# A decoder layer on one core: the merge of the attention heads as four pairs of seven block products, with the weights' sums and the split w_out made ahead

## The chip, the cores and the metric

The kernel runs on one core of one Trainium2 chip. The metric is device time in microseconds (us): the median of the runs of the whole program, all stages in one launch. Five engines work side by side on that core, each through its own queue of instructions in order: TensorE (PE, matrix products; PEld is its loading of stationary blocks), VectorE (DVE), ScalarE (ACT), GpSimd (POOL) and SyncE (SP, which here only issues DMAs). Matrix products accumulate in PSUM banks of 128 x 512 floats; everything else lives in SBUF, 128 partitions wide, and in device memory (the tiles whose names end in `_d`).

## The reference

One layer, 1024 tokens, width 1024, float32 throughout. What matters here is the middle of it:

```python
proj = h @ w_in                                  # q, k, v, pooled branch, memory query, gate logits
a = diff_attention(q_d, k_d, v_d, lam)           # 8 heads of 128 channels
a = rms_norm(a, subln_g) * (1.0 - lam_init)      # per head
y_attn = a.reshape(B, S, 1024) @ w_attn_branch   # "the merge of the heads"
...
gates = sigmoid(gate_logits).reshape(B, S, 3, D)
mix = gates[:, :, 0] * y_attn + gates[:, :, 1] * y_pool + gates[:, :, 2] * y_mem
x = x + rms_norm(mix @ w_out, norm_mix_post)
h2 = rms_norm(x, norm_ffn_pre)                   # then w_up, a causal conv, gelu, w_down
```

## The kernel before

Products are made in float32 precision out of three passes: each operand is split into a high part (`F32R`, the rounded value) and a low part (the rest), and `mm3` (L102) issues high x high, high x low, low x high. `split` (L85) is one ACT copy and one DVE subtraction. Activations are held transposed: channels on the 128 partitions, tokens along the row, in two halves of H = 512 tokens.

Several large products already use a scheme of seven block products in place of eight: a product of a 2 x 2 block matrix of weights by a 2 x 2 block matrix of activations (two halves of the contracted channels, two halves of the tokens) is made of seven products of sums of blocks. `seven` (L198) does so for a pair of 128-channel output tiles: `weight_sums` (L184) makes four sums of weight blocks on DVE, `product` (L175) splits one 128 x 512 block of weights into a page (tags `wh` and `wl`, two of each, so four pages) and runs 4 x 3 matmuls with one of the operands B11, T1, T2, B22, T3, B21, T4; results are combined as the banks `pa`, `pb`, `pc` are emptied.

The order of the work is not that of the source alone. A planner goes through all instructions with a cost model before the program is built; on each engine it takes, among those that it believes ready, the one written earliest. `tc.issue_after(ins)` puts what follows behind `ins` on its engine. Tiles rotate in pools by tag, so an instruction also waits until the tile whose place it takes has been read for the last time. Once the order is fixed, each engine keeps it on the chip: an instruction that waits holds up all behind it on that engine. The same holds for the DMA issues on SP.

The stages that the change touches, in order:

- **The mix gates' stage** (L860 to L881). For four pairs of output tiles and two branches, `seven` makes gate logits from the stream's operands; the sigmoid is multiplied with `y`, a branch's output that was loaded from memory, and the sum goes to `mixp_d`. Tag `y` has two places of 8 KB a partition. The weights come as two raw tiles an iteration (L868).
- **The attention** (L1156 and on), heads in turn. `weigh_values` sends each head's output to `ao_d`, `head_norm` its sum of squares to `ss_d`; `turn_sums` (L1243) sends the softmax sums to `sum_d`. For heads 4 to 7 `load_norms(1)` (L1251) reads both back, `head_norms(1)` (L1258) makes the norm factors on DVE in small steps and writes `r_d`. Meanwhile PE makes the last three tiles of attention gate logits (`gate`, L1112, dt 5 to 7).
- **The merge.** For each head the loop at L1373 loads its output `a` and its norm factors `rb`, spread over all partitions, multiplies them (L1384) and splits the result into `ath`, `atl`. `merge_heads` (L1356) makes an output tile of 128 channels: 8 heads x 3 matmuls for each half of the tokens; the first two tiles take heads 0 to 3 while heads 4 to 7 still come in. `merge` (L1403) multiplies with the gate, adds `mixp_d` and splits the result into `mixh`, `mixl`. `load_wo` (L1396) loads and splits w_out's eight row blocks.
- **The w_out stage** (L1482). For eight tiles of 128 tokens, 8 x 2 x 3 matmuls, then both norms, then the rows are turned and, for the second half of the tokens, the feed-forward operands B21 and B11 are split (`early_operands`, L1453).
- **The feed-forward's first products** (`early_products`, L1533), which need only B21; the other operands are made meanwhile (`late_operands`, L1466).

## Time and profile before

| | |
|---|---|
| median of three runs | 1726.82 us (1725.88 to 1727.25) |
| span of the profiled execution (its only time) | 1727.6 us |
| PE busy | 1712.8 us, 99% |
| DVE, ACT, POOL busy | 1241.3, 886.6, 45.0 us |
| mean TensorE clock granted | 0.999 |
| matmuls of the merge (tile pya) | first at 910.8 us, last at 997.6 us |
| w_out's matmuls (tile pout) | first at 997.9 us, last at 1090.1 us |
| DMA moved | 294.41 MB, mean 170 GB/s |

In the profile, L12 is line 12 of the kernel before, `out<-in` names tiles by the program's names, and times of places are counted from the start of the span. A group's row gives durations of one instruction (min/median/max in ns) and the first and the last start. Matmuls are pipelined: one takes longer from start to end than the step from one to the next. What stands in square brackets on a row of the timeline is how long the engine sat idle before it and what released it. "DMA to landing" is the time from the issue to the last byte.

### The profile page before, as it was taken

What the parts mean: (1) busy time and instruction counts of PE and PEld (TensorE: products, weight loads), DVE (VectorE), ACT (ScalarE), POOL (GpSimd) and SP (SyncE); (2) the same over time, 40 slices, a digit from 0 to 9 for tenths busy, and PEclk for the clock granted to TensorE, in tenths of its full rate; (3) what the DMA queues carried; (4) which work ended last, traced back from release to release, by engine and by line L of the source; (5) the groups of instructions that cost most, each with busy time, mean ns of one, the idle gap of its engine ahead of it and who ended that gap; (6) DMA issues with size and microseconds to landing.
All of it is one profiled execution on the core that took longest, in us unless ns stands there. A gap on an engine that the chain in (4) does not pass through costs nothing.

```text
span 1727.6 us, 22400 instructions
## 1 busy us (share of the span) xinstructions
PE 1712.8 (99%) x8106; PEld 1421.4 (82%) x8106; DVE 1241.3 (72%) x2047; ACT 886.6 (51%) x1577; POOL 45.0 (3%) x103
## 2 busy tenths in 40 slices
...
PEclk9999999999999999999999999999999999999999
...
GB/s 273 317 281 114 163 150 133 166 147 143 266 237 159 201 231 170 176 182 152 145 187 239 176 230 50 171 225 92 124 112 107 122 85 98 190 299 106 107 149 142
DMA packets 232803, 294.41 MB, mean 170 GB/s; under 512 B 15865, under 2 KB 161526, under 8 KB 230006
## 3 DMA queue, kind: packets, MB, share of 16 engines
...
q8 instruction: 64, 1.05, 0.3%
q14 instruction: 45, 0.37, 0.1%
q10 hardware_dynamic: 16, 0.00, 0.0%
...
## 4 chain that ended last, share of the span: by engine, by line
PE 91%; DVE 5%; DMA 2%; ACT 1%; issue 1%; SPq 0%; DVEq 0%; ACTq 0%
PE pa L103 8%; PE pa L104 8%; PE pa L105 8%; PE pb L103 5%; PE pb L104 5%; PE pb L105 5%; PE pss L1161 3%; PE poa L1217 2%; PE pd L103 2%; PE pd L105 2%; PE pd L104 2%; PE pe L105 2%; PE pe L104 2%; PE pe L103 2%; PE pout L103 2%; PE pout L105 2%
## 5 line engine op out<-in xcount | busy, mean ns | idle before, releaser
L89 ACT ACTIVATE wpage<-s 128x512 fp32r<-128x512 f32 x136 | 85.3, 627 | 108.2 <-DVE s L188 35.3
L90 DVE TENSOR_TENSOR wpage<-s,wpage 128x512 fp32r<-128x512 f32 x136 | 92.8, 688 | 43.2 <-ACT wpage L89 43.2
L1565 DVE SCALAR_TENSOR_TENSOR cvt<-gv,cols,cvt 128x1023 f32<-128x1023 f32 x88 | 112.5, 1278 | 15.6 <-ACT cvt L1561 14.9
L1165 DVE CUSTOM_DVE_ANT_0 z<-pss,hbias 128x256 f32<-128x256 f32 (+7 forms) x128 | 94.5, 752 | 26.0 <-PE pss L1161 24.8
L1170 ACT ACTIVATE z<-z,mx 128x256 f32<-128x256 f32 (+7 forms) x128 | 98.8, 773 | 20.8 <-DVE mx L1165 20.7
L103 PE MATMUL pa<-T,wpage 128*128 128x512 f32 x264 | 102.8, 389 | 0.0
L105 PE MATMUL pa<-T,wpage 128*128 128x512 f32 x264 | 102.7, 389 | 0.0
L104 PE MATMUL pa<-T,wpage 128*128 128x512 f32 x264 | 102.7, 389 | 0.0
L1161 PE MATMUL pss<-ks,q 128*128 128x512 f32 (+5 forms) x384 | 86.6, 349 | 1.4 <-DVE mx L1165 1.4
L89 ACT ACTIVATE page<-blk 128x1024 fp32r<-128x1024 f32 (+1 forms) x42 | 41.4, 989 | 85.7 <-PE pe L104 50.6
L90 DVE TENSOR_TENSOR page<-blk,page 128x1024 fp32r<-128x1024 f32 (+1 forms) x42 | 47.5, 1130 | 38.1 <-ACT page L89 38.1
L1161 PEld LDWEIGHTS pss<-ks,q 128*128 128x128 f32 x384 | 62.9, 189 | 11.1 <-DVE mx L1165 6.2
L103 PE MATMUL pd<-page 128*128 128x512 f32 x176 | 68.7, 390 | 0.0
L104 PE MATMUL pd<-page 128*128 128x512 f32 x176 | 68.5, 389 | 0.0
L105 PE MATMUL pd<-page 128*128 128x512 f32 x176 | 68.3, 389 | 0.0
L103 PE MATMUL pa<-hT,wpage 128*128 128x512 f32 x168 | 65.5, 390 | 0.1
L105 PE MATMUL pa<-hT,wpage 128*128 128x512 f32 x168 | 65.4, 389 | 0.0
L104 PE MATMUL pa<-hT,wpage 128*128 128x512 f32 x168 | 65.4, 389 | 0.0
L1217 PEld LDWEIGHTS poa<-aT,v 128*128 128x128 f32 x480 | 60.7, 190 | 3.0 <-ACT srow L1237 1.4
L1217 PE MATMUL poa<-aT,v 128*128 128x256 f32 (+1 forms) x480 | 62.5, 280 | 0.0
L103 PEld LDWEIGHTS pa<-T,wpage 128*128 128x128 f32 x264 | 49.6, 188 | 10.7 <-DVE gv L250 0.3
L104 PEld LDWEIGHTS pa<-T,wpage 128*128 128x128 f32 x264 | 49.6, 188 | 10.2
...
## 6 DMA issues: line engine op xcount, KB each, us to landing
...
wd<-in_w_down_dram SPq DMA_DIRECT2D x22, 512.0 KB, 5.0
tw_d<-wd SPq DMA_DIRECT2D x11, 1024.0 KB
rawv<-in_w_up_dram SPq DMA_DIRECT2D x22, 512.0 KB, 5.8
rawu<-in_w_up_dram SPq DMA_DIRECT2D x22, 512.0 KB, 4.1
ff_d<-cvt SPq DMA_DIRECT2D x22, 512.0 KB, 5.4
blk<-ff_d SPq DMA_DIRECT2D x20, 512.0 KB, 7.9
br<-tw_d SPq DMA_DIRECT2D x20, 512.0 KB, 5.0
```

Source lines behind the costliest of these rows:

```text
L89: copy = nc.scalar.activation(out=hi, in_=src, func=AF.Copy)
L90: nc.vector.tensor_tensor(out=lo, in0=src, in1=hi.bitcast(F32), op=ALU.subtract)
L103: nc.tensor.matmul(o, ah, bh, start=first, stop=False, skip_group_check=onto)
L104: nc.tensor.matmul(o, ah, bl, start=False, stop=False, skip_group_check=onto)
L105: return nc.tensor.matmul(o, al, bh, start=False, stop=last, skip_group_check=onto)
L1161: last["scores"] = nc.tensor.matmul(pss[:, i * H:i * H + m], q[:, j, c, ts], keys, start=(j == 0), stop=(j == 1))
L1165: nc.vector.tensor_tensor_reduce(out=halves(z[:, 0:n]), in0=pss.rearrange("p (a m) -> p a m", a=2)[:, 0:parts, 0:m], in1=halves(biases[h][ ...
L1170: nc.scalar.activation(out=z[:, 0:n], in_=z[:, 0:n], func=AF.Exp, scale=-1.0, bias=mx[:, c:c + 1], accum_out=sm if c else sums[:, h, t:t + 1])
L1217: nc.tensor.matmul(po[:, qs], (vh, vl)[i][:, k, :], w[j][:, ws], start=(n == 0), stop=(n == len(terms) - 1))
L1565: nc.vector.scalar_tensor_tensor(out=cv[:, sh:], in0=u[:, 0:S - sh], scalar=w, in1=cv[:, sh:], op0=ALU.mult, op1=ALU.add)
```

## The change

The merge becomes, for each of four pairs of output tiles, seven block products over heads 0 to 3 and 4 to 7 and over the two halves of the tokens: B11 and T1 (of heads 0 to 3 alone), T2, B22, T3, B21, T4. `merge_begin` runs the first two products of a pair, `merge_rest` the other five. Three pairs begin before anything of heads 4 to 7 is used. The operands are made head by head from the normed outputs: 28 splits of 128 x 512 where there were 16 halves, and sixteen subtractions, eight on DVE and eight on POOL. The loads of `a` and `rb` for heads 0 to 3 now stand ahead of `load_norms(1)`; for heads 4 to 7 `rb` has one place, and `a` shares six places with heads 0 to 3.

The four sums of blocks of w_attn_branch that a pair needs (`merge_sums`), and w_out's split parts (`split_wo`), are made in the gates' stage and written through POOL's DMA queue to `mw_d` and `wo_d`; both take places of tag `y`. The merge reads its sums, and the w_out stage its split parts, back from there. `mix` is kept as f32 and split tile by tile in the w_out stage. There, B11's split moves from `early_operands` to `late_operands`. The `sum_d` write moves from SP to ACT.

```diff
@@ -318,6 +318,8 @@
     wk_d = dram.tile([NH, P, 2, KT, P], F32, name="wk_d")
     v_d = dram.tile([NH, P, 2, KT, P], F32, name="v_d")
     tw_d = dram.tile([CH, P, 2, 2, H], F32, name="tw_d")
+    mw_d = dram.tile([H4, P, 4, H4, P], F32, name="mw_d")
+    wo_d = dram.tile([KT, P, 2, D], F32, name="wo_d")
     ss_d = dram.tile([NH, S], F32, name="ss_d")
...
@@ -859,6 +861,28 @@
     bstack.close()
     with tc.tile_pool(name="gp", reuse_waits="tile", bufs=2, side="right") as gp_:
+        def split_wo(k):
+            w = gp_.tile([P, 2, D], F32R, tag="y", name="wo")
+            raw = w[:, 1].bitcast(F32)
+            nc.sync.dma_start(out=raw, in_=w_out[k * P:(k + 1) * P, :])
+            split(w[:, 0], w[:, 1], raw)
+            nc.gpsimd.dma_start(out=wo_d[k], in_=w.bitcast(F32))
+        def merge_sums(p):
+            m = gp_.tile([P, 4, H4, P], F32, tag="y", name="ms")
+            for e in range(2):
+                nc.sync.dma_start(out=m[:, 2 * e:2 * e + 2].rearrange("p a k c -> p (a k) c"),
+                                  in_=chunk(w_attn_branch, (2 * p + e) * P))
+            a11, a12, a21, a22 = [m[:, j] for j in range(4)]
+            for o, x0, x1, op in ((a22, a21, a22, ALU.add), (a21, a11, a21, ALU.subtract),
+                                  (a11, a22, a11, ALU.subtract), (a12, a12, a11, ALU.subtract)):
+                nc.vector.tensor_tensor(out=o, in0=x0, in1=x1, op=op)
+            nc.gpsimd.dma_start(out=mw_d[p], in_=m)
+        ahead_of_merge = {0: (0, "0"), 1: (1, 2), 2: (3, "1"), 3: (4, "2"), 4: (5, 6), 5: (7, "3")}
         for dt in range(0, KT, 2):
             mix = None
             for b in (1, 0):
@@ -874,6 +898,8 @@
                 seven(raws, (s12[:, 0], s12[:, 1], s43[:, 0], s43[:, 1]), hop, g)
                 sigmoid = nc.scalar.activation(out=g, in_=g, func=AF.Sigmoid)
                 nc.vector.tensor_tensor(out=g, in0=g, in1=y, op=ALU.mult)
+                for what in ahead_of_merge.get(dt + 1 - b, ()):
+                    merge_sums(int(what)) if isinstance(what, str) else split_wo(what)
                 if b == 1:
                     mix = g
                 else:
@@ -1246,13 +1272,14 @@
...
-        nc.sync.dma_start(out=sum_d[g * HG:(g + 1) * HG].rearrange("h (t p) -> (h t) p", p=P), in_=row)
+        nc.scalar.dma_start(out=sum_d[g * HG:(g + 1) * HG].rearrange("h (t p) -> (h t) p", p=P), in_=row)
     def load_norms(g):
         st = small.tile([P, 4, HG, 8], F32, tag="hn", name="hn", bufs=1)
         for src, r in ((ss_d, 0), (sum_d, 3)):
-            nc.sync.dma_start(out=st[:, r], in_=src[g * HG:(g + 1) * HG].rearrange("h (p f) -> p h f", f=8))
+            with tc.issue_after(marks["head"].ins) if g else nullcontext():
+                nc.sync.dma_start(out=st[:, r], in_=src[g * HG:(g + 1) * HG].rearrange("h (p f) -> p h f", f=8))
         hns[g] = st
     def head_norms(g):
@@ -1342,84 +1369,202 @@
...
+    cstack.close()
+    dstack = ExitStack()
+    sub = dstack.enter_context(tc.tile_pool(name="sub", reuse_waits="tile", bufs=6, side="right"))
+    opr = dstack.enter_context(tc.tile_pool(name="opr", reuse_waits="tile", bufs=1, side="right"))
+    estack = ExitStack()
+    ope = estack.enter_context(tc.tile_pool(name="ope", reuse_waits="tile", bufs=1, side="right"))
+    mops = {}
+    def operands(pool, names, tag=None):
+        for n in names:
+            mops[n] = pool.tile([P, 2, H4, H], F32R, tag=tag or n, name="m" + n)
+    def mop(n, k):
+        return mops[n][:, 0, k, :], mops[n][:, 1, k, :]
+    def split_mop(n, k, src):
+        split(*mop(n, k), src)
+    operands(ope, ("B11", "T1"))
+    operands(opr, ("B22", "T2"))
+    rstack = ExitStack()
+    rbp = rstack.enter_context(tc.tile_pool(name="rbp", reuse_waits="tile", bufs=4, side="left"))
+    gs = sub.tile([P, 1], F32, name="gs", bufs=1)
+    nc.vector.tensor_scalar(out=gs, in0=cols[:, 1, 44:45], scalar1=1.0 - LAM_INIT, scalar2=None, op0=ALU.mult)
+    heads = {}
+    def load_head(h):
+        a = sub.tile([P, S], F32, tag="a", name="a")
+        nc.sync.dma_start(out=a, in_=ao_d[h])
+        rb = (rbp if h < H4 else sub).tile([P, S], F32, tag="rb", name="rb", bufs=4 if h < H4 else 1)
+        marks["head"] = nc.sync.dma_start(out=rb, in_=r_d[h:h + 1, :].partition_broadcast(P))
+        heads[h] = a, rb
+    def normed_head(h):
+        if h not in heads:
+            load_head(h)
+        a, rb = heads[h]
+        with tc.issue_after(ends["square"].ins):
+            nc.vector.scalar_tensor_tensor(out=a, in0=a, scalar=gs, in1=rb, op0=ALU.mult, op1=ALU.mult)
+        heads[h] = a[:, 0:H], a[:, H:S]
+    def upper_operands(k):
+        b11, b12 = heads[k]
+        split_mop("B11", k, b11)
+        nc.vector.tensor_tensor(out=b12, in0=b12, in1=b11, op=ALU.subtract)
+        split_mop("T1", k, b12)
+    def lower_operands(k):
+        (b11, t1), (_, b22) = heads[k], heads[H4 + k]
+        split_mop("B22", k, b22)
+        nc.vector.tensor_tensor(out=b22, in0=b22, in1=t1, op=ALU.subtract)
+        split_mop("T2", k, b22)
+    def third_operand(k):
+        (b11, _), (_, t2) = heads.pop(k), heads[H4 + k]
+        nc.gpsimd.tensor_tensor(out=b11, in0=t2, in1=b11, op=ALU.subtract)
+        split_mop("T3", k, b11)
+    def last_operands(k):
+        b21, t2 = heads.pop(H4 + k)
+        split_mop("B21", k, b21)
+        nc.gpsimd.tensor_tensor(out=b21, in0=b21, in1=t2, op=ALU.subtract)
+        split_mop("T4", k, b21)
+    for k in range(H4):
+        load_head(k)
     load_norms(1)
-    cstack.close()
...
-            split(ath[h], atl[h], a)
+    for dt in range(5, KT):
+        for step in steps(gate(dt), 8):
+            step()
+    for k in range(H4):
+        normed_head(k)
+        upper_operands(k)
+    with tc.issue_after(ends["square"].ins):
+        head_norms(1)
+    for k in range(2):
+        normed_head(H4 + k)
+        lower_operands(k)
+    rstack.close()
     hstack.close()
     mstack = ExitStack()
     mpool = mstack.enter_context(tc.tile_pool(name="mh", reuse_waits="tile", bufs=4, side="left"))
-    mixh = [mpool.tile([P, KT, H], F32R, tag="big", name="mixh%d" % i) for i in range(2)]
-    mixl = [mpool.tile([P, KT, H], F32R, tag="big", name="mixl%d" % i) for i in range(2)]
+    mix = [mpool.tile([P, KT, H], F32, tag="big", name="mix%d" % i) for i in range(2)]
+    operands(mpool, ("B21", "T4"), "big")
     wostack = ExitStack()
+    operands(wostack.enter_context(tc.tile_pool(name="opt", reuse_waits="tile", bufs=1, side="left")), ("T3",))
+    HALVES = {"B11": 0, "B21": 1, "T4": 3}
+    SUMS = {"T2": 0, "B22": 1, "T3": 2, "T1": 3}
+    def merge_weights(p, names):
+        w = wst.tile([P, 2, H4, P], F32, tag="raw", name="rawm", bufs=2)
+        for j, n in enumerate(names):
+            if n in SUMS:
+                src = mw_d[p, :, SUMS[n]]
+            else:
+                e, part = divmod(HALVES[n], 2)
+                src = w_attn_branch[part * H:part * H + H, (2 * p + e) * P:(2 * p + e + 1) * P].rearrange(
+                    "(k p) c -> p k c", p=P)
+            nc.sync.dma_start(out=w[:, j], in_=src)
+        return {n: w[:, j] for j, n in enumerate(names)}
+    def corners(p):
+        return [mix[i][:, 2 * p + e, :] for e in range(2) for i in range(2)]
+    pas = {}
+    def merge_begin(p):
+        if p == 2:
+            both = bank2(name="pm")
+            pa, pb = both[:, 0:H], both[:, H:2 * H]
+        else:
+            pa, pb = pbank(name="pm"), bank(name="pm")
+        pas[p] = pa, pb
+        c11, _, c21, _ = corners(p)
+        ws = merge_weights(p, ("B11", "T1"))
+        product(ws["B11"], mop, "B11", pa)
+        nc.scalar.activation(out=c11, in_=pa, func=AF.Copy)
+        product(ws["T1"], mop, "T1", pb)
+        nc.scalar.activation(out=c21, in_=pb, func=AF.Copy)
+    def gated(p, e, i, c, src=None):
+        hs = slice(i * H, (i + 1) * H)
+        gm = sub.tile([P, 2, H], F32, tag="a", name="gm")
+        nc.sync.dma_start(out=gm[:, 0], in_=gate_d[2 * p + e][:, hs])
+        nc.sync.dma_start(out=gm[:, 1], in_=mixp_d[2 * p + e][:, hs])
+        nc.scalar.activation(out=gm[:, 0], in_=gm[:, 0], func=AF.Sigmoid)
+        nc.vector.tensor_tensor(out=c, in0=c if src is None else src, in1=gm[:, 0], op=ALU.mult)
+        nc.vector.tensor_tensor(out=c, in0=c, in1=gm[:, 1], op=ALU.add)
+    def merge_rest(p, names, between=lambda j: None):
+        pa, pb = pas.pop(p)
+        c11, c12, c21, c22 = corners(p)
+        ws = {}
+        for j, n in enumerate(names):
+            if j % 2 == 0:
+                ws = merge_weights(p, names[j:j + 2])
+            acc = bank2(name="pc")[:, 0:H] if n == "B21" else pb if n == "B22" else pa
+            product(ws[n], mop, n, acc, n == "B21")
+            if n == "T2":
+                nc.scalar.activation(out=c12, in_=pa, func=AF.Copy)
+            elif n == "B22":
+                nc.vector.tensor_tensor(out=c12, in0=pb, in1=c12, op=ALU.add)
+                gated(p, 0, 1, c12)
+            elif n == "T3":
+                nc.vector.tensor_tensor(out=c22, in0=pa, in1=c21, op=ALU.add)
+                gated(p, 1, 1, c22)
+            elif n == "T4":
+                gated(p, 1, 0, c21, pa)
+            else:
+                nc.vector.tensor_tensor(out=c11, in0=acc, in1=c11, op=ALU.add)
+                gated(p, 0, 0, c11)
+            between(j)
+    woh, wol = {}, {}
+    def load_wo(k, tile):
+        woh[k], wol[k] = tile[:, 0], tile[:, 1]
+        nc.sync.dma_start(out=tile.bitcast(F32), in_=wo_d[k])
+    for p in range(3):
+        merge_begin(p)
+    for k in range(2):
+        third_operand(k)
+    for k in range(2, H4):
+        normed_head(H4 + k)
+        lower_operands(k)
+        third_operand(k)
+    for k in range(H4):
+        last_operands(k)
+    EARLY, LATE = ("T2", "B22", "T3", "B21", "T4"), ("B21", "T2", "T3", "T4", "B22")
+    merge_rest(0, EARLY)
+    merge_begin(3)
+    estack.close()
     woa = wostack.enter_context(tc.tile_pool(name="woa", reuse_waits="tile", bufs=1, side="left"))
-    woh, wol = [], []
...
-        load_wo(woa, k)
+    def first_wo(k):
+        load_wo(k, woa.tile([P, 2, D], F32R, name="wo%d" % k))
+    merge_rest(1, EARLY, lambda j: first_wo(j // 2) if j in (1, 3) else None)
+    merge_rest(2, EARLY, lambda j: first_wo(2 + j // 2) if j in (1, 3) else None)
+    def second_wo(j):
+        if j in (1, 3):
+            pair = mpool.tile([P, 2, 2, D], F32R, tag="big", name="wop")
+            for e in range(2):
+                load_wo(3 + j + e, pair[:, e])
+    merge_rest(3, LATE, second_wo)
     dstack.close()
     gstack.close()
@@ -1453,7 +1598,6 @@
...
-        split_op("B11", F[0][:, 0:H4, cs], cs=cs)
...
@@ -1467,6 +1611,7 @@
         cs, (b11, b21, b12, b22) = late_blocks(c, n)
         split_op("T1", b12, cs=cs)
+        split_op("B11", b11, cs=cs)
         split_op("B22", b22, cs=cs)
...
@@ -1475,9 +1620,7 @@
...
-    with tc.tile_pool(name="wo", reuse_waits="tile", bufs=1, side="right") as wo:
-        for k in range(4, KT):
-            load_wo(wo, k)
+    with tc.tile_pool(name="ml", reuse_waits="tile", bufs=2, side="right") as ml:
         late = None
...
@@ -1486,17 +1629,19 @@
...
+            hl = ml.tile([P, 2, KT, P], F32R, tag="hl", name="hl")
+            for ks in ((slice(0, 6), slice(6, KT)) if t == 0 else (slice(0, KT),)):
+                split(hl[:, 0, ks], hl[:, 1, ks], mix[i][:, ks, c:c + P])
             po = bank2(name="pout")
             for k in range(KT):
                 for j in range(2):
                     hs = slice(j * H, (j + 1) * H)
-                    mm3(po[:, hs], mixh[i][:, k, c:c + P], mixl[i][:, k, c:c + P],
+                    mm3(po[:, hs], hl[:, 0, k, :], hl[:, 1, k, :],
                         woh[k][:, hs], wol[k][:, hs], k == 0, k == KT - 1)
             if late:
                 turn_rows(*late)
             if t == 4:
                 operand(mpool, "B21")
-                operand(mpool, "B11")
             if t == 7:
                 late_difference(0, 2)
             y = yp.tile([P, D], F32, tag="y", name="y", bufs=3)
@@ -1541,7 +1686,7 @@
...
-    for n, pool in (("T1", mpool), ("B22", mpool), ("T2", tpool), ("T3", tpool), ("T4", tpool)):
+    for n, pool in (("T1", mpool), ("B11", mpool), ("B22", mpool), ("T2", tpool), ("T3", tpool), ("T4", tpool)):
         operand(pool, n)
     for c0 in range(0, 8, 2):
         early_products(c0)
```

54 lines of the change are left out of this document (1 added, 53 removed).

## The prediction

> **What bounds the kernel now.** I read the page first: busy shares, the granted clock, the chain that ended last.
>
> ```profile
> span 1727.6 us, 22400 instructions
> PE 1712.8 (99%) x8106; PEld 1421.4 (82%) x8106; DVE 1241.3 (72%) x2047; ACT 886.6 (51%) x1577; POOL 45.0 (3%) x103
> PEclk9999999999999999999999999999999999999999
> PE 91%; DVE 5%; DMA 2%; ACT 1%; issue 1%; SPq 0%; DVEq 0%; ACTq 0%
> ```
>
> PE is busy in 99% of the span, makes up 91% of the chain, and its clock is never cut. But the average says nothing of the stages that change, so the second view is the table of stretches: the mix gates' stage (260 to 413), the last gates with the heads' loads (878 to 911), the merge (911 to 998), the w_out stage (998 to 1091), the first products of w_up (1091 to 1151). One saturated stretch stands with them.
>
> ```profile
> core 0: us, PE busy (x) PEld busy (x) DVE busy (x) ACT busy (x) POOL busy (x), PEclk, DMA share, GB/s
> 900.00:910.00 10.00, 10.00 (x46) 8.28 (x45) 7.88 (x7) 4.17 (x5) 1.08 (x2) 1.00 0.99 355
> ...
> 878.00:911.00 33.00, 33.00 (x159) 27.44 (x159) 17.14 (x30) 11.87 (x18) 4.29 (x8) 1.00 0.73 257
> 911.00:998.00 87.00, 87.00 (x385) 72.03 (x385) 50.69 (x62) 35.20 (x48) 0.54 (x1) 1.00 0.62 208
> 998.00:1091.00 93.00, 93.00 (x440) 77.52 (x439) 51.34 (x98) 38.58 (x75) 0.00 (x0) 1.00 0.37 120
> 1091.00:1151.00 60.00, 60.00 (x272) 49.80 (x271) 40.04 (x62) 37.39 (x67) 0.00 (x0) 1.00 0.66 210
> 260.00:413.00 153.00, 152.85 (x673) 125.97 (x672) 92.26 (x119) 65.72 (x98) 0.00 (x0) 1.00 0.41 135
> ```
>
> PE has no gap from 878 to 1151, and 0.15 us of gaps in the gates' stage. So a matmul removed is time removed, and every new wait of PE is time added; DVE and ACT work costs nothing as long as it is in time. The price of a matmul is not its 389 ns, since matmuls overlap. It is the pitch, from the merge's own rows.
>
> ```profile
> L103 PE MATMUL pya<-ath,wh x128: 389/389/389, 910.8 to 997.2; 128*128 128x512 f32 x128
> L105 PE MATMUL pya<-ath,wl x128: 389/389/389, 911.3 to 997.6; 128*128 128x512 f32 x128
> ```
>
> 384 matmuls (128 on each of three lines) start from 910.8 to 997.6: 86.8 / 383 = 0.2266 us each.
>
> **The merge itself.** Before: 8 channel tiles x 2 halves x 8 heads x 3 = 384 matmuls. After: 4 pairs x 7 products x 4 blocks x 3 = 336, of the same shape. 48 x 0.2266 = **10.9 us less**. This is certain as far as PE stays fed; the count follows from the code. The rest is what may open a gap. The small prices:
>
> ```profile
> L89 ACT ACTIVATE wpage<-s 128x512 fp32r<-128x512 f32 x136 | 85.3, 627 | 108.2 <-DVE s L188 35.3
> L90 DVE TENSOR_TENSOR wpage<-s,wpage 128x512 fp32r<-128x512 f32 x136 | 92.8, 688 | 43.2 <-ACT wpage L89 43.2
> ...
> L1384 DVE SCALAR_TENSOR_TENSOR a<-a,gs,rb x8: 1277/1281/1284, 893.6 to 919.7; 128x1024 f32<-128x1024 f32 x8
> ...
> L89 ACT ACTIVATE woh<-rawo x8: 1042/1052/1062, 971.4 to 1002.1; 128x1024 fp32r<-128x1024 f32 x8
> L90 DVE TENSOR_TENSOR wol<-rawo,woh x8: 1218/1219/1226, 972.5 to 1004.5; 128x1024 fp32r<-128x1024 f32 x8
> ```
>
> **Gates' stage, added work.** Eight splits of w_out (DVE 1.22, ACT 1.05) and 16 sums of w_attn_branch blocks (DVE 0.69): DVE 9.8 + 11.0 = 20.8 us, so 113 of 153; ACT 8.4, so 74 of 153. DMA: w_out 8 x (0.5 MB in, 1 MB out) and the sums 4 x (1 in, 1 out) = 20 MiB, 21 MB, or 137 GB/s over 153 us beside the 135 there: 272, a share near 0.83. Room on average; what counts is the one place where PE already waits:
>
> ```profile
> 321.23 3.09 SPq L868 DMA_DIRECT2D rawg<-in_w_in_dram  x2
> ...
> 328.91 0.69 DVE L188 TENSOR_TENSOR s<-rawg 128x512 f32<-128x512 f32 x1 [2.75 <-DMA rawg<-in_w_in_dram]
> 329.52 0.68 DVE L217 TENSOR_TENSOR g<-pa,g 128x512 f32<-128x512 f32 x1
> ...
> 329.81 0.39 PE L105 MATMUL pc<-hTh,wpage 128*128 128x512 f32 x1
> 330.35 0.47 PE L103 MATMUL pa<-hT,wpage 128*128 128x512 f32 x1
> ...
> 312.42 1.28 DVE L90 TENSOR_TENSOR wpage<-s,wpage 128x512 fp32r<-128x512 f32 x2
> ...
> 319.36 0.60 ACT L211 ACTIVATE g<-pb 128x512 f32<-128x512 f32 x1 [1.51 <-PE pb L105]
> ...
> rawg<-in_w_in_dram SPq DMA_DIRECT2D x16, 512.0 KB, 5.3
> y<-branch_d SPq DMA_DIRECT2D x8, 1024.0 KB, 5.2
> ```
>
> DVE takes its queue in order. There s (L188) waits for the second raw page; behind it stands the add L217, which must empty bank pa before T4's product may go on in it; PE's step from 329.81 to 330.35 is 0.54 in place of 0.23, a gap of 0.31. In the iteration before, T1's page is done at 313.1 (the first of the two from 312.42) and its product, which ends at 319.36 and lasts 12 x 0.2266, starts at 316.6: 3.5 us in hand. The new loads share SP's queue with these pages, the new writes go by POOL's. The loads of sums (1 MB when the slot "y" comes free) stand about where a y load (1 MB) stood, so pages do not come behind more than before; the writes do run into them. Bounds: 0 if pages land in 5.3 as now, and the rival below if they land as in a full queue. I take 0.3 us in three more of the iterations, 0.9 us, near the low end, because the share stays under 0.9.
>
> **Heads' stage.** Before, a head cost DVE 1.28 + 1.22. After, 8 x 1.28, 28 operand splits x 0.69 and 8 subtractions x 0.69 on DVE = 35.1 us (20.0 before), 28 x 0.63 = 17.6 on ACT, 8 subtractions on POOL. PE needs the operands in this order, from the gates' end at 910.8: B11 and T1 for three pairs, 72 matmuls, 16.3 us; T2 from 927.1 (its fourth block at 929.1), B22 929.8, T3 932.6, B21 935.3, T4 938.0. DVE has, from the attention's end (883.5) to 938, the 35.1, eleven weight pages (7.6), two gate pages (2.4) and head_norms (3.3): 48.4 of 54.5. Enough, if inputs come in time. The chain for heads 4 to 7:
>
> ```profile
> L1161 PE MATMUL pss<-ks,q x96: 221/341/504, 805.0 to 866.5; 128*128 128x384 f32 x24, 128*128 128x512 f32 x24, 128*128 128x320 f32 x16, 128*128 128x448 f32 x16
> ...
> L1255 SPq DMA_DIRECT2D hn<-ss_d x1: 359/359/359, 886.9 to 886.9; - x1
> L1267 SPq DMA_DIRECT2D r_d<-hn x1: 371/371/371, 895.5 to 895.5; - x1
> ...
> 903.49 0.33 SPq L1383 DMA_DIRECT2D rb<-r_d  x1
> ...
> DMA to landing us min/median/max: 8.2/9.0/9.9
> ...
> DMA to landing us min/median/max: 4.4/4.5/4.6
> sum_d<-trow SPq DMA_DIRECT2D x2, 16.0 KB, 2.4
> ```
>
> (The landings are rb's and rawo's.) Now r_d is written at 895.5 and the first rb that needs it leaves at 903.5, 8 us later, behind 4 MB of heads 0 to 3 in a full queue. In the change those eight loads stand ahead of load_norms(1) on SP, in memory that the scores leave at 866.5 or that was free; 4.2 MB at 355 GB/s are 11.8 us, done before 886.9. Moving the sum_d write from SP to ACT (0.37 us of issue at most) clears SP's queue for them; ACT's is half empty. So r_d needs about 2.4 us to land, rb of head 4 leaves at about 898. From there the rb's go through one buffer: landing 4.5 + issue 0.5 + 1.28 = 6.3 us each, 4 heads 25, then subtraction and two splits 2.7: T2's last block at 926, three us before its use. Bounds: that (cost 0) and landings of 9.0: 18 us later, 15 late. Near 4.5, since then only 4 MB go in 27 us beside the small pages. I take 0, with the rival below. POOL's subtractions: 128x512 with two inputs does not occur in the trace; the nearest rows are
>
> ```profile
> 591.96 1.09 POOL L1045 IOTA bias<- 128x1152 f32 x1 [548.36 <-PE pa L105]
> ...
> 593.16 1.61 POOL L1047 TENSOR_SCALAR_AFFINE_SELECT bias<-bias 128x1152 f32<-128x1152 f32 x1
> ```
>
> 0.48 by the first, 0.72 by the second and its double for a second input, 1.4; 8 x 1.4 = 11 us, spread over the same 25: 0 on the path either way.
>
> **Merge and w_out stage.** Weight pages: 28 pairs of splits (17.6 ACT, 19.3 DVE) for 8 x (1.06, 1.22) before, plus 24 evictions; mix's and w_out's splits leave. DVE's sum here goes from 50.7 by -11.0 - 9.8 - 9.8 + 19.3 + 8.3 to 48 of 76 us, the operands above apart: 0. The last pair runs B21, T2, T3, T4, B22: T3 goes on in T2's bank and T4 in T3's, with no product between. The eviction between is 0.60 to 0.69 by the rows
>
> ```profile
> L213 ACT ACTIVATE g<-pa x8: 598/598/600, 265.0 to 398.9; 128x512 f32<-128x512 f32 x8
> L217 DVE TENSOR_TENSOR g<-pa,g x8: 682/691/692, 270.4 to 404.4; 128x512 f32<-128x512 f32 x8
> ```
>
> plus about 0.25 to hand over: 1.8 us at most for both, 0 if the planner slips B22's matmuls between. I take 0.9. w_out's blocks 6 and 7 can load only after T4 leaves its tile; cover is B22 (2.7) and 36 matmuls (8.2), 10.9 us, against 5.2 for the first MB and 3.0 more for the second at 355 GB/s: 0, at most 3 if x's loads crowd in. In w_out's stage eight mix splits come in (DVE 9.8) and B11's leaves (2.8): 58 of 93, one row ahead: 0. B11's late split adds 2.6 to DVE's 40.0 of 60: 0; at most 2.6 where it delays a page. For these small edits together I take 0.6.
>
> **Sum.** -10.9 + 0.9 + 0.9 + 0.6 = -8.5 us. Against the profile's span, 1727.6 - 8.5 = 1719.1; the runs' median 1726.82 is 0.8 below that span (the execution has no other time than its span), so **1718.3**.
>
> **Rivals.**
> *Late heads.* With heads 0 to 3 already there at 883.5, DVE has 13.4 us of first-half operands ready, traced ahead of head_norms(1); if the planner puts the 16 small steps of the norms (3.3) and a gate page (1.2) behind them, r_d goes out at 901.4 in place of 895.5, rb of head 4 at 904, and T2's last block is ready at 931.9: 2.8 us late; with landings of 5.3 it is 6.0. For it: DVE is the busiest of the helpers there. Against: now the norms' steps run in DVE's waits. Time: 1718.3 + 4.4 = 1722.7.
> By the Trainium skill's TensorE: Matmul & The Clock Gate, Part 1, "What's actually happening", an idle window of about 3.4 us halves the PE clock until a busy one has passed. As an estimate from that page, a 6 us gap in one piece would cost 1.7 more, 1724.4; the profile's clock row is full everywhere and no run here shows it.
> *Slower: pages of the gates' stage land late.* If the added 21 MB make rawg land as rb does in a full queue (9.0), it comes 3.7 later; four iterations in which the add stands behind s lose all of it, three others have about 3 in hand (3.5 by the rows above): 4 x 3.7 + 3 x 0.7 = 17 us, 1726.8 - 10.9 + 17 + 1.5 = 1734. It makes the kernel slower by more than 0.2% from a landing of 8.5 on. For it: the writes of 1 MB fall where pages are under way. Against: a share of 0.83, not 0.99.
> The Trainium skill's DMA: Bandwidth & Descriptors, "Issuing engines are not separate DMA queues", speaks for it: DMAs of all issuers run on the same 16 engines, so POOL's queue shields nothing. The 355 GB/s row is of SP's loads alone and cannot show it.
> *Nothing waits.* All three small terms are 0: 1726.8 - 10.9 = 1716.
>
> **Chances.** Forecast 0.55, late heads 0.22, slower 0.08, nothing waits 0.15. The measurement can tell about 0.2%, 3.5 us: faster means under 1723.4. That takes the first and last cases and six tenths of the late heads: 0.83; same 0.11, the rest of them and the gates' stage's milder half; slower 0.06. The range, 1713.5 to 1726, takes in the late heads and, below, 2.5 us of what a new order of the queues may give.
>
> **What would show it.** Right: 336 matmuls of the merge at 0.227 over about 76 us; the first rb of head 4 to 7 leaving before 900; rawg landing under 6.5; PE full from 878 to 1140. Wrong: PE waiting on T2's split (late heads), on L217 or the weight pages near 300 to 400 (the slower case), on the copies between T2, T3, T4 for more than 2 us, or on wo's last load.

## The result, and the profile after

The changed kernel takes 1754.96 us (median of four runs, 1753.55 to 1755.75) beside 1727.03 for the kernel before in the same session: ratio 1.0158 (95% interval 1.0143 to 1.0172). It was forecast at 1718.3. The profiled execution's span is 1754.0, 34.9 above the 1719.1 of the sum.

The page of the changed kernel (span, busy shares, chain of waits):

```profile
span 1754.0 us, 22575 instructions
PE 1716.4 (98%) x8058; PEld 1412.9 (81%) x8058; DVE 1283.2 (73%) x2115; ACT 905.0 (52%) x1621; POOL 65.1 (4%) x123
...
PE 79%; DVE 8%; DMA 7%; issue 3%; ACT 2%; SPq 1%; POOL 0%; DVEq 0%; ACTq 0%; POOLq 0%
```

PE still looks full. But its share of the chain has gone from 91 to 79%; DVE (5 to 8%) and DMA (2 to 7%) have taken most of it. A few groups say in which stage, by their first and last start: the stream's products (`pa<-hT`), the attention gates (`pg`) and w_up's first products (`pa<-B`). First the kernel before, then the changed one:

```profile
L103 PE MATMUL pa<-hT,wpage x168: 387/389/467, 262.0 to 601.9; 128*128 128x512 f32 x168
L105 PE MATMUL pg<-hTh,wl x96: 387/389/499, 603.1 to 910.6; 128*128 128x512 f32 x96
L103 PE MATMUL pa<-B,wpage x132: 389/389/476, 1091.1 to 1494.0; 128*128 128x512 f32 x132
```

```profile
L103 PE MATMUL pa<-hT,wpage x168: 389/389/499, 261.1 to 618.8; 128*128 128x512 f32 x168
L105 PE MATMUL pg<-hTh,wl x96: 387/389/497, 619.9 to 926.9; 128*128 128x512 f32 x96
L103 PE MATMUL pout<-wo,hl x64: 389/389/501, 1021.6 to 1109.5; 128*128 128x512 f32 x64
L103 PE MATMUL pa<-B,wpage x132: 389/389/476, 1116.4 to 1519.3; 128*128 128x512 f32 x132
...
L892 SPq DMA_DIRECT2D rawg<-in_w_in_dram x16: 367/381/5977, 170.3 to 398.2; - x16
DMA to landing us min/median/max: 4.0/8.7/13.3
```

The last of the stream's L103 matmuls starts 16.9 us later (618.8 against 601.9) where 0.9 was forecast: 16.0 too many, lost before the attention begins. From the gates' end (pg's last start) to the first product of w_up it is 189.5 us against 180.5, where 171.1 were forecast: 18.4 too many. Together that is 34.4 of the 34.9 (by the medians the miss is 36.7). The merge's products are as many as forecast, 336, but they take from 927.1 to w_out's start at 1021.6: 94.5 us in place of 76.

Stretches of the changed kernel, columns as in the table of before:

```profile
core 0: us, PE busy (x) PEld busy (x) DVE busy (x) ACT busy (x) POOL busy (x), PEclk, DMA share, GB/s
260.00:413.00 153.00, 140.74 (x593) 111.95 (x592) 100.98 (x129) 64.39 (x93) 6.57 (x12) 0.98 0.75 256
...
310.00:320.00 10.00, 7.07 (x30) 5.59 (x30) 2.68 (x5) 0.63 (x1) 0.00 (x0) 0.96 0.95 342
320.00:330.00 10.00, 9.64 (x36) 7.15 (x35) 7.72 (x9) 7.51 (x11) 0.53 (x1) 0.87 0.51 175
...
940.00:950.00 10.00, 4.78 (x13) 2.80 (x12) 9.09 (x11) 7.05 (x13) 4.57 (x4) 0.69 0.67 213
950.00:960.00 10.00, 8.65 (x29) 6.55 (x28) 9.72 (x10) 7.24 (x12) 4.45 (x3) 0.80 0.53 176
```

In the gates' stage PE is idle for 12.3 us; DVE has 101 busy us of 153, so its sum has room. The mean DMA share is 0.75, less than the 0.83 that I reckoned, yet 0.95 where PE stood. From 940 to 960, 42 matmuls start where 88 fit at 0.2266: 10.4 us lost, more than half of what the merge lost.

Both places on the timeline of the changed kernel, rows picked from several engines:

```profile
305.76 6.39 SPq L892 DMA_DIRECT2D rawg<-in_w_in_dram  x2
316.18 0.39 PE L105 MATMUL pa<-hTh,wpage 128*128 128x512 f32 x1
318.01 0.69 DVE L188 TENSOR_TENSOR s<-rawg 128x512 f32<-128x512 f32 x1 [6.15 <-DMA rawg<-in_w_in_dram]
319.50 0.80 PE L103 MATMUL pb<-hT,wpage 128*128 128x512 f32 x1 [2.93 <-ACT wpage L89]
320.09 0.63 PE L104 MATMUL pb<-hT,wpage 128*128 128x512 f32 x1
320.56 0.80 PE L105 MATMUL pb<-hT,wpage 128*128 128x512 f32 x1
...
919.41 0.36 SPq L1294 DMA_DIRECT2D r_d<-hn  x1
926.83 1.28 DVE L1414 SCALAR_TENSOR_TENSOR a<-a,gs,rb 128x1024 f32<-128x1024 f32 x1 [7.45 <-DMA rb<-r_d]
936.87 2.83 POOL L1437 TENSOR_TENSOR a<-a 128x512 f32<-128x512 f32 x1 [4.89 <-DVE mB L90]
939.73 1.89 ACT L89 ACTIVATE mT<-a 128x512 fp32r<-128x512 f32 x3 [3.21 <-POOL a L1437]
940.91 2.42 DVE L90 TENSOR_TENSOR mT<-a,mT 128x512 fp32r<-128x512 f32 x2 [2.37 <-ACT mT L89]
942.75 0.61 ACT L89 ACTIVATE wpage<-rawm 128x512 fp32r<-128x512 f32 x1
943.42 0.50 PE L103 MATMUL pm<-mT,wpage 128*128 128x512 f32 x1 [2.12 <-ACT wpage L89]
946.77 0.79 PE L103 MATMUL pm<-mB,wpage 128*128 128x512 f32 x1 [2.47 <-ACT wpage L89]
```

At 318 DVE stands 6.15 us at s (L188) for the second raw page, as in the rival; PE's next matmul comes 3.3 us after the last. At 940 the weight page that PE wants stands on ACT behind an operand's copy, which waits for a subtraction on POOL. And after a gap the matmuls step by about 0.45 in place of 0.23 for a while, with a PEclk of 0.87 from 320 to 330: the half clock.

### The profile page after: what moved, and what is told of

Its sections match the earlier page's. It is cut to its first block, busy times and chain, and to the rows that moved or that the text cites. A ratio compares the mean times of both kernels' runs of the same rounds, so it can differ in the third digit from the quotient of the medians.

```text
span 1754.0 us, 22575 instructions
## 1 busy us (share of the span) xinstructions
PE 1716.4 (98%) x8058; PEld 1412.9 (81%) x8058; DVE 1283.2 (73%) x2115; ACT 905.0 (52%) x1621; POOL 65.1 (4%) x123
## 4 chain that ended last, share of the span: by engine, by line
PE 79%; DVE 8%; DMA 7%; issue 3%; ACT 2%; SPq 1%; POOL 0%; DVEq 0%; ACTq 0%; POOLq 0%
PE pa L103 6%; PE pa L105 6%; PE pa L104 6%; PE pb L103 4%; PE pb L104 4%; PE pb L105 4%; PE pss L1187 3%; PE poa L1243 2%; PE pd L103 2%; PE pd L104 2%; PE pd L105 2%; DMA rawg<-in_w_in_dram 2%; PE pe L104 2%; PE pe L103 2%; PE pe L105 2%
## 5 line engine op out<-in xcount | busy, mean ns | idle before, releaser
L1191 DVE CUSTOM_DVE_ANT_0 z<-pss,hbias 128x256 f32<-128x256 f32 (+7 forms) x128 | 94.5, 752 | 25.8 <-PE pss L1187 24.7
L1196 ACT ACTIVATE z<-z,mx 128x256 f32<-128x256 f32 (+7 forms) x128 | 98.9, 774 | 20.8 <-DVE mx L1191 20.4
L103 PE MATMUL pa<-T,wpage 128*128 128x512 f32 x264 | 102.9, 390 | 0.3 <-DVE gv L250 0.3
L103 PE MATMUL pa<-hT,wpage 128*128 128x512 f32 x168 | 66.1, 394 | 4.0 <-DVE g L217 2.5
L103 PE MATMUL pd<-page 128*128 128x512 f32 x176 | 68.7, 390 | 0.0
L103 PEld LDWEIGHTS pa<-T,wpage 128*128 128x128 f32 x264 | 49.6, 188 | 11.4 <-DVE gv L250 0.8
```

The source lines that it names most:

```text
L103: nc.tensor.matmul(o, ah, bh, start=first, stop=False, skip_group_check=onto)
L1191: nc.vector.tensor_tensor_reduce(out=halves(z[:, 0:n]), in0=pss.rearrange("p (a m) -> p a m", a=2)[:, 0:parts, 0:m], in1=halves(biases[h][ ...
L1196: nc.scalar.activation(out=z[:, 0:n], in_=z[:, 0:n], func=AF.Exp, scale=-1.0, bias=mx[:, c:c + 1], accum_out=sm if c else sums[:, h, t:t + 1])
```

## The experiments

"Gates" is the start of the stream's last L103 matmul (601.9 before), "merge" the time from the last gate matmul to the first w_up product (180.5 before), both from the one profiled execution, while the median is over all runs. The ratio is to the kernel before on the same chip.

| kernel | median us | ratio (95%) | gates | merge |
|---|---|---|---|---|
| the change | 1754.96 | 1.0158 (1.0143 to 1.0172) | 618.8 | 189.5 |
| gates_only | 1746.53 | 1.0098 (1.0069 to 1.0127) | 619.6 | 180.8 |
| gates_no_writes | 1728.63 | 1.0004 (0.9992 to 1.0015) | 601.4 | 180.7 |
| writes_from_elsewhere | 1748.89 | 1.0116 (1.0087 to 1.0145) | 622.7 | 180.5 |
| writes_1kb_rows | 1754.24 | 1.0147 (1.0117 to 1.0177) | 628.9 | 180.5 |
| wo_split_in_merge | 1754.96 | 1.0147 (1.0117 to 1.0176) | 599.6 | 208.4 |
| subs_on_dve | 1752.14 | 1.0130 (1.0101 to 1.0160) | 617.7 | 187.1 |
| wo_split_own_places | 1742.56 | 1.0079 (1.0050 to 1.0109) | 601.5 | 194.8 |
| norms_in_three | 1746.17 | 1.0100 (1.0071 to 1.0130) | 600.8 | 198.2 |
| no_pool_subtractions | 1736.99 | 1.0054 (1.0035 to 1.0074) | 602.3 | 186.1 |
| no_low_parts | 1741.61 | 1.0076 (1.0047 to 1.0105) | 601.9 | 192.5 |
| norms_first_subs_on_dve | 1744.57 | 1.0093 (1.0064 to 1.0123) | 601.9 | 195.7 |
| first_rows_early | 1736.37 | 1.0050 (1.0020 to 1.0079) | 601.5 | 188.1 |
| seven_places | 1730.39 | 1.0012 (1.0002 to 1.0021) | 603.4 | 180.4 |
| seven_places_pool | 1736.93 | 1.0049 (1.0034 to 1.0063) | 601.6 | 188.1 |
| banks_and_rows | 1728.41 | 1.0000 (0.9990 to 1.0010) | 601.3 | 183.1 |
| gates_by_pool | 1732.00 | 1.0021 (1.0012 to 1.0030) | 601.4 | 183.8 |
| gate_behind_pages | 1725.23 | 0.9986 (0.9977 to 0.9995) | 602.6 | 177.6 |
| halves_by_pool | 1729.56 | 1.0011 (1.0003 to 1.0020) | 600.5 | 182.4 |

**The gates' stage: who is late?** The kernel before with the change's additions to this stage and nothing that reads them; then the same without the two writes.

```diff
+                for what in ahead_of_merge.get(dt + 1 - b, ()):
+                    merge_sums(int(what)) if isinstance(what, str) else split_wo(what)
```

> The kernel before with only the added work of the gates' stage: w_out's splits and the weights' sums are made and written to memory, and nothing reads them (its output is the reference's). Theory: the gates' stage loses by itself, independent of the merge, because its pages land late: last matmul of the stage's products some 16 us later than before, whole kernel 1727 + 16 = 1743, rawg landing near 8.7 us. Rival, that the loss comes from the planner laying the whole program out anew for the other merge: under 1732.

```diff
-            nc.gpsimd.dma_start(out=wo_d[k], in_=w.bitcast(F32))
...
-            nc.gpsimd.dma_start(out=mw_d[p], in_=m)
```

> As the kernel before with the added loads, DVE and ACT work of the gates' stage, but without the two writes to memory (12 of the 20 MB are left out, the results are used by nothing). Theory (bytes in flight delay the pages): most of the loss is gone, 1727 + 0 to 5, rawg landing under 7 us. Rival (DVE's and ACT's added 20.8 and 8.4 us get in the way of the pages): still 1738 or more, with rawg landing as in the kernel before.

The stretch 260 to 413 and rawg's landing, first with the writes, then without:

```profile
260.00:413.00 153.00, 142.58 (x597) 113.52 (x596) 101.63 (x130) 64.61 (x94) 6.57 (x12) 0.97 0.74 255
...
DMA to landing us min/median/max: 3.9/8.3/13.2
```

```profile
260.00:413.00 153.00, 152.78 (x674) 126.04 (x673) 110.60 (x142) 73.99 (x105) 0.00 (x0) 1.00 0.59 189
...
DMA to landing us min/median/max: 4.0/4.5/8.1
```

All 20.8 us of DVE work, ACT's copies and 8 MiB of loads cost nothing: DVE is at 110.6 of 153 and PE full. The 12.6 MB of writes carry the loss, 18 us. Two ways are left: the written bytes crowd the pages out, or a write holds a place of tag y, SP stands at the next load for that place, and the pages stand behind it (in gates_only's waits of SP's queue, total, times and longest):

```profile
SPq L868 <- DMA mw_d<-ms: 21.3, 3, 8.5
```

To tell them apart, the same number of bytes was written out of a tile that nobody waits for; and the true bytes in rows of 1 KB in place of 8.

```diff
-            nc.gpsimd.dma_start(out=wo_d[k], in_=w.bitcast(F32))
+            write_still(w[:, 0, 0:1].bitcast(F32), wo_d[k].rearrange("p a c -> p (a c)"))
...
+            copy = nc.gpsimd.tensor_copy(out=c, in_=seen)
+            with tc.issue_after(copy.ins):
+                nc.gpsimd.dma_start(out=dst, in_=hTh[0][:, 0:4].rearrange("p k c -> p (k c)").bitcast(F32))
```

> The kernel before with all that the change adds to the gates' stage, read by nothing later; but the twelve writes of 1 MB take their bytes from a tile that nobody overwrites (one half of the stream's high parts), each sent when its made tile's first column can be read, so that they carry the wrong numbers and hold no place of tag y. Theory of bytes (the written 12.6 MB crowd the raw pages out of the DMA engines): as in the kernel with the true writes, 1746, landing of rawg 8 us and more. Theory of places (SP stands at a load for a place of tag y that a write still holds, 56 us in sum in that stage, and the raw pages stand behind it in SP's queue): 1727 to 1731, landing of rawg back near 4.5 to 6.

```diff
-    wo_d = dram.tile([KT, P, 2, D], F32, name="wo_d")
+    wo_d = dram.tile([KT, 8, P, 2 * P], F32, name="wo_d")
```

> The same additions with the true writes, but laid out in memory in rows of 1 KB in place of 8 KB a partition; read by nothing later. Theory of bytes, in the form that few large packets (7.3 KB) starve the pages' packets of 512 bytes: faster than the 1746 with 8 KB rows, 1730 to 1738. Bytes alone: 1746. Theory of places: 1746 or up to 3 more, since a place is held at least as long.

The loss stays without the places (1748.89; gates at 622.7, 20.8 us late): the theory of places falls, that of bytes stands. Its sign was only half met: rawg lands at a median of 7.1 (at most 9.1) where it said 8 and more. Smaller packets make it worse (1754.24, landing 9.9), so it isn't that the writes' packets are large. How much writing the stage bears was bracketed only: the 4.2 MB of the sums alone (next run, where w_out's loads are gone too) cost nothing, 12.6 MB cost 18 us. Whether the same writes would cost as much from SP's or ACT's queue was not run.

**Does it help to split w_out in the merge?** Its rows are loaded raw and split there; the sums stay in the gates' stage. In the second form they go through tag a, not through the two places of the weight pages, and the splits of the last five blocks are traced behind the merge.

```diff
-        nc.sync.dma_start(out=tile.bitcast(F32), in_=wo_d[k])
+        raw = wst.tile([P, D], F32, tag="raw", name="rawo", bufs=2)
+        nc.sync.dma_start(out=raw, in_=w_out[k * P:(k + 1) * P, :])
+        split(tile[:, 0], tile[:, 1], raw)
```

> The changed kernel with one part undone: w_out is loaded raw and split in the merge, as before; the weights' sums stay in the gates' stage. That takes 12 of 20 MB and 9.8 us of DVE out of the gates' stage and 4 of 8 MB out of the merge. Theory of bytes: the gates' stage loses 4 us or less, and the merge's last third has fewer waits, so 1755 - 13 - 3 = 1739. Rival (DVE work): half of the gates' loss stays and the merge gets slower by DVE's 9.8 us there, 1747 or more.

```diff
-        raw = wst.tile([P, D], F32, tag="raw", name="rawo", bufs=2)
+        wor[k] = sub.tile([P, D], F32, tag="a", name="rawo")
```

> The changed kernel, but w_out is not split in the gates' stage: its rows are loaded in the merge into places of tag a and split there, the last five traced behind the merge; the weights' sums stay in the gates' stage. Gates' stage: 0 to 1 us over the kernel before. Theory that the two gaps of 5.8 and 6.8 us in the earlier form were ACT's split standing in front of the weight pages: they go, the last gate matmul to the first w_up product takes 190 us or less, and the time is 1733 to 1738 (1727 and the 9 to 10 us which the merge of the changed kernel is longer than that of the kernel before). Rival, that w_out's splits do not fit beside the pages at all (DVE and ACT short): gaps of 5 us and more near the last pair, 1745 or more.

The gates' stage is whole again (599.6, 601.5). The first form was expected at 1739 and gave it all back in the merge (208.4), with two gaps of 5.8 and 6.8 us; the second has none of that size, but is at 194.8, 5 over the 190 that I expected. From here on the question is the merge alone.

**POOL, DVE or the norms?** Four edits, each at one suspect. The first stands on the changed kernel, the others on wo_split_own_places. The last edit is for all operands but B11 and T1.

```diff
-        nc.gpsimd.tensor_tensor(out=b11, in0=t2, in1=b11, op=ALU.subtract)
+        nc.vector.tensor_tensor(out=b11, in0=t2, in1=b11, op=ALU.subtract)
```

> The changed kernel with POOL's eight subtractions on DVE. In the changed kernel's trace DVE's 128x512 splits take up to 1.78 us instead of 0.69 while POOL subtracts. Theory A: that slowing holds T2, T3 and T4's operands back, so without it DVE's splits are 0.69 again, the operands are done some 5 us earlier and the kernel is at 1751. Theory B: the heads' loads (r_d late, one buffer for rb) set the end; DVE waits for them anyway, and the time stays within 2 us of 1755.

```diff
+    GROUPS = ((0, 4), (4, 7), (7, 8))
...
+            if h in (HG, 7) and b == 0:
+                stages.append(lambda g=h // 7: turn_sums(g))
```

> As wo_split_own_places, and the norm factors of heads 4 to 6 are made during head 7's attention, so that at the end only head 7's are late. Theory that the norms' chain makes T2 late (r_d written at 903.7 in the time of before): rb of head 4 lands before 900, no PE gap over 1 us between 925 and 955 of the changed kernel's time, 8 to 12 us less than wo_split_own_places: 1722 to 1728. Rival, that the single place of rb and the DVE steps slowed by POOL (128x512 splits of 1.78 us in place of 0.69) make it late anyway: less than 4 us gained, with gaps where T2's or T3's splits end.

```diff
-        nc.gpsimd.tensor_tensor(out=b11, in0=t2, in1=b11, op=ALU.subtract)
...
-        nc.gpsimd.tensor_tensor(out=b21, in0=b21, in1=t2, op=ALU.subtract)
```

> wo_split_own_places (1742.6) with the eight subtractions on POOL left out, so that T3 and T4 are split from tiles without them (this leaves out part of the computation). Nothing else moves to another engine. Theory of POOL (its 1.3 to 2.8 us each hold up ACT's next copy, the weight pages behind it, and DVE's steps, 1.78 in place of 0.69): the gaps of 2.57, 3.01, 1.43 and 1.94 us between 923 and 943 shrink to less than half, the half clock there goes, 6 to 9 us faster: 1734 to 1737. Theory of late heads (rb and the norms' chain, whatever POOL does): less than 3 us faster.

```diff
-        split(*mop(n, k), src)
+        if n in ("B11", "T1"):
+            split(*mop(n, k), src)
+        else:
+            nc.scalar.activation(out=mop(n, k)[0], in_=src, func=AF.Copy)
```

> wo_split_own_places (1742.6) without the twenty DVE subtractions that make the low parts of B22, T2, T3, B21 and T4; the high part is used in both places, so matmuls and ACT's copies are as many as before (this leaves out part of the computation). It takes 20 x 0.69 = 13.8 us of DVE time out of the stretch from 905 to 945. Theory that DVE has no room in that stretch: the gaps there shrink by more than half, 5 us or more faster, 1738 or less. Theory of late heads or of POOL's latency: less than 3 us faster, gaps ended by ACT behind POOL as now.

With the subtractions on DVE the changed kernel gained 2.8 us by the medians and 0.28% by the ratios (4.8 us), whose intervals overlap. That is some of POOL's price, between the two theories. Earlier norms gained nothing (1746.17 against 1742.56), though r_d for heads 4 to 6 went out at 877.2 in place of 902.0; 13.8 us less DVE work gained 1. So DVE's room was not short, and the norms' chain alone was not the cause. Leaving POOL out gained 5.6 (4.3 by the ratios). The low parts' group on DVE shows one part of the reason, first in the changed kernel, then without POOL:

```profile
L90 DVE TENSOR_TENSOR mT<-a,mT x16: 624/679/1817, 903.8 to 960.2; 128x512 fp32r<-128x512 f32 x16
...
L1431 POOL TENSOR_TENSOR a<-a x4: 1305/1504/1795, 930.6 to 955.6; 128x512 f32<-128x512 f32 x4
L1437 POOL TENSOR_TENSOR a<-a x4: 1277/1720/2827, 936.9 to 957.4; 128x512 f32<-128x512 f32 x4
```

```profile
L90 DVE TENSOR_TENSOR mT<-a,mT x16: 622/683/691, 888.1 to 936.4; 128x512 fp32r<-128x512 f32 x16
```

A step of 0.68 takes up to 1.82 while POOL subtracts; the other part is ACT's queue, shown above. How the price divides between them was not measured.

**What the rest waits for.** norms_in_three with head 7's norm steps traced first and the subtractions on DVE; then also with the first 128 rows of mix split into places of their own.

```diff
+    with tc.issue_after(ends["square"].ins):
+        head_norms(2)
     for dt in range(5, KT):
```

> norms_in_three (1746.2) with head 7's norm steps traced ahead of the first half's operands and with POOL's subtractions on DVE. If both causes hold (late inputs, and POOL), the gaps of 6.5 and 2.4 us between 922 and 934 go, and with them the half clock: 1735 to 1738. If DVE's own room is what lacks, the 5.5 us which the subtractions add there come back as gaps: 1740 to 1746.

```diff
-            hl = ml.tile([P, 2, KT, P], F32R, tag="hl", name="hl")
...
+    hl0 = [sub.tile([P, KT, P], F32R, tag="a", name="hl0") for _ in range(2)]
```

> norms_first_subs_on_dve, and the first 128 tokens of mix are split for w_out into two places of tag a, in place of a new tile that lies where operand B22 of the last product lay. Theory that this tile's memory makes w_out start late (the three gaps of 1.35, 0.92 and 1.43 us and a half clock behind them): 4 to 6 us less than norms_first_subs_on_dve. Rival, that the chain behind T4 (two adds, two splits) sets it: 0 to 2 us less.

The first gained 1.6 and so fell among the times that I had put down to a lack of DVE room, against which no_low_parts speaks; the true wait was on neither list. The second gained 8.2, more than expected. The tile `hl` lies where operand B22 of the last product lies, so its split had to wait for that product; with places of its own, the three gaps at the start of w_out's stage (1.5, 0.9 and 1.7 us) are gone. Two things limit this reading: the edit also traces that split earlier, and in the profiled executions only 4.4 of the 7.6 us lie in w_out's stage (98.7 to 94.3), the rest ahead of it. What was still late stood in its trace:

```profile
910.27 1.11 SPq L1400 DMA_DIRECT2D a<-ao_d  x2
...
910.96 0.69 DVE L90 TENSOR_TENSOR wpage<-rawm,wpage 128x512 fp32r<-128x512 f32 x1
916.07 1.28 DVE L1410 SCALAR_TENSOR_TENSOR a<-a,gs,rb 128x1024 f32<-128x1024 f32 x1 [4.43 <-DMA a<-ao_d]
```

DVE is idle just before the rush, because head 6 can be loaded only when `third_operand` gives up a place of tag a. So the places were dealt out anew, and then POOL was put back:

```diff
-    sub = dstack.enter_context(tc.tile_pool(name="sub", reuse_waits="tile", bufs=6, side="right"))
+    sub = dstack.enter_context(tc.tile_pool(name="sub", reuse_waits="tile", bufs=7, side="right"))
...
+    ah = load_halves(1)
```

> first_rows_early (1736.4) with the places dealt out anew: all eight rb go through the four places of heads 0 to 3, the freed one becomes a seventh place of a, and heads 6 and 7 load first only the half that T2 and B22 need, both in one place, without waiting for third_operand. Theory of places (DVE and ACT stood idle from 911 to 917 because the a of head 6 could be loaded only after T3's first operand, so everything of heads 6 and 7 came in one heap): the gaps of 1.6, 3.2 and 1.8 us from 923 to 931 and the half clock there go, 7 to 10 us faster: 1727 to 1730. Rival, that ACT and DVE lack room between 917 and 935 in any case: less than 3 us faster.

> seven_places with the eight subtractions for T3 and T4 back on POOL. If POOL's price is the queue behind it (ACT's copies wait for its 1.3 to 2.8 us, DVE's steps take 1.78 in place of 0.69) and not the lateness of the heads, it comes back here: 3 to 6 us slower than seven_places. If POOL hurt only where the inputs were late: within 1.5 us of it.

Six us gained (7 to 10 were expected), and 6.5 lost again with POOL: POOL's price is its own and does not need late inputs.

**The last 10 us.** T4's bank, the first rows' place and the queue of w_up's pages; then the gates held back behind the next product's pages; then the late halves by POOL's queue, or all gate loads by it.

```diff
-                gated(p, 1, 0, c21, pa)
+                nc.scalar.activation(out=c21, in_=pa, func=AF.Copy)
+                gated(p, 1, 0, c21)
```

> seven_places (1730.4), and: T4's product leaves its bank by an ACT copy in place of DVE's multiplication by the gate (which holds the bank until the gate has come from memory); the first rows of mix are split into T3's tile, free after the third product of the last pair; and w_up's first pages are loaded behind the rows of x for the first 512 tokens. Theory that the gaps left in seven_places come from a bank, a place and a queue held too long (2.5 us and a half clock near 945, 1.9 and 0.9 us near 1020): 5 to 7 us faster, 1723 to 1726, which is faster than the kernel before. Rival, that the loads themselves are late (the DMA share there is 0.85 to 1.05), and the waits move to the next instruction: 0 to 2 us faster.

```diff
-        nc.sync.dma_start(out=gm[:, 0], in_=gate_d[2 * p + e][:, hs])
+        nc.gpsimd.dma_start(out=gm[:, 0], in_=gate_d[2 * p + e][:, hs])
```

> banks_and_rows with the loads of gate_d and mixp_d in the merge issued by POOL in place of SP. Theory that SP's waits for places (6.4 and 3.5 us in one group of weight loads) hold up these loads: 1 to 3 us faster than banks_and_rows. Rival, that the 16 DMA engines are what is short: no difference within 1 us, or slower, since nothing then holds these loads back behind the weights.

```diff
-        nc.scalar.activation(out=gm[:, 0], in_=gm[:, 0], func=AF.Sigmoid)
+            with tc.issue_after(page.ins) if page else nullcontext():
+                nc.scalar.activation(out=gm[:, 0], in_=gm[:, 0], func=AF.Sigmoid)
```

> banks_and_rows (1728.4), with the sigmoid and the product of a gated output held back behind the pages of the next product, for the first three pairs; its loads stay where they are. Theory that what is left of the gaps in the merge (2.9 and 1.3 us near 925, 2.0, 1.1 and 2.2 us from 963 to 982, and a half clock behind the first) comes from ACT and DVE standing at a gate that is still on its way, with a page or a bank's release behind: 4 to 7 us faster, 1721 to 1725, faster than the kernel before. Rival, that the weight pages' own loads are late by then: 0 to 2 us faster.

> gate_behind_pages, and the second halves of heads 6 and 7 with their norms are loaded through POOL's queue, so that they do not stand behind three weight loads which SP holds for 7.4 us (DVE waited 1.6 us for them). Expected 0 to 2 us faster than gate_behind_pages; slower by 1 us or more if the loads sent earlier crowd out the weight pages.

banks_and_rows gained 2.0 where 5 to 7 were expected: PE's waits moved on. At the largest gap that is left, a gate stands on ACT (924.23), but the page that PE waits for is held by DVE: its low part (926.01) comes after a head's multiplication, which waits for late norms (`rh`). The gate's wait holds up the copies behind it on ACT:

```profile
923.61 1.28 DVE L1577 SCALAR_TENSOR_TENSOR ah<-ah,gs,rh 128x1024 f32<-128x1024 f32 x1 [1.62 <-DMA rh<-r_d]
924.23 1.28 ACT L1524 ACT_TABLE_LOAD   x1 [2.17 <-DMA gm<-gate_d]
926.01 0.68 DVE L90 TENSOR_TENSOR wpage<-rawm,wpage 128x512 fp32r<-128x512 f32 x1
926.75 0.50 PE L105 MATMUL pm<-mT,wpage 128*128 128x512 f32 x1 [2.54 <-DVE wpage L90]
```

Sending the gates' loads by POOL was 3.6 us slower: there they wait for places of tag a instead (five waits, 26.9 us in all, for DVE's last step on a gated output), so SP's queue was not what made them late. Holding the sigmoid back behind the pages gained 3.2, under the 4 to 7 expected. ACT's waits for a gate load and the stretch 910 to 1000, first in banks_and_rows, then in gate_behind_pages:

```profile
ACT gm L1524 <- DMA gm<-gate_d: 13.9, 9, 3.2
...
910.00:1000.00 90.00, 82.64 (x339) 64.38 (x339) 64.61 (x98) 48.66 (x83) 0.54 (x1) 0.96 0.75 238
```

```profile
ACT gm L1527 <- DMA gm<-gate_d: 4.6, 3, 2.7
...
910.00:1000.00 90.00, 86.25 (x363) 68.47 (x362) 69.31 (x105) 52.78 (x86) 0.54 (x1) 0.98 0.75 237
```

That kernel, gate_behind_pages, is a little faster than the kernel before: 0.9986 of it (0.9977 to 0.9995), 2.5 us. Of the 10.9 us of saved matmuls, 2.9 show in its merge (177.6 for 180.5); two gaps of 2.1 and 2.5 us, the clock (0.98 over 90 us, 1.8) and a longer step of the matmuls (1.3, below) take most of the rest. These figures come from its profiled execution, which at 1728.5 us was the longest of eleven (median 1725.23). halves_by_pool was 4.3 slower, the side that its expectation gave to loads sent earlier that crowd out the weight pages. Its trace says something else:

```profile
924.94 1.28 DVE L1590 SCALAR_TENSOR_TENSOR ah<-ah,gs,rh 128x1024 f32<-128x1024 f32 x1 [2.62 <-DMA rh<-r_d]
926.25 1.15 ACT L89 ACTIVATE mB<-ah 128x512 fp32r<-128x512 f32 x2 [3.38 <-DVE ah L1590]
```

The loads did not leave earlier: `rh` went out by POOL at 917.9 in place of 916.8 by SP. DVE waits 2.62 us for it (1.48 in gate_behind_pages), ACT stands behind DVE, and the weight page (928.00) stands behind ACT's copies: this is the gap of 5.8 us at 922.9. The gap of 2.1 us in gate_behind_pages is the same wait, so the late halves' norms are next in line there; that was not tried.

## Why the prediction was wrong, by its own steps

- **The 48 matmuls, −10.9.** The count holds. The step is a little longer than the 0.2266 taken (below): some 1.3 us less gain. The condition beside it, that PE stays fed, is what failed.
- **The gates' stage, +0.9.** This step failed: 16.9 us in the change, 18 by itself. I chose the low bound "because the share stays under 0.9". The share did: 0.75. But a mean over 153 us is no measure of a page that comes while 1 MB is being written; at 310 to 320 the share is 0.95, and pages land up to 13.3 us after their issue. The rival *pages of the gates' stage land late* is what came: landing 8.7 where it put 9.0 and its turning point at 8.5, loss 16.9 where it put 17. I gave it 0.08. That the loss agrees so closely is in part luck: the rival put it all at the add L217, where PE stands only 2.5 of its 12.3 idle us; more goes to weight pages and bank copies on ACT (single steps of up to 3.3 us), and about 3 us to the clock (0.98 over 153 us). The Trainium skill says in DMA: Bandwidth & Descriptors, "Issuing engines are not separate DMA queues", that DMAs started by different engines run on the same 16 DMA engines and interleave there. The trace agrees: the writes went by POOL's queue and SP's pages were late by them.
- **The heads, 0.** This failed too: 10.4 us lost between 940 and 960. The first links of *late heads* came as written (r_d at 919.41, less the 16.3 of the stage before, is 903.1 for 901.4; rb of head 4 left at 921.88, so 905.6 for 904). But its price, 4.4, was that of one chain, and putting that chain right gained nothing. Four things stood behind each other: POOL's subtractions, the places of a, the gates in the queues of ACT and DVE, the norms. The last was not taken back alone at the end, so what it is worth in seven_places is open; in gate_behind_pages a wait for late norms still costs a gap of 2.1 us.
- **POOL's subtractions, 0.48 to 1.4 each and 0 on the path.** This failed as well, and the 0 had no more reason than that they are spread out. They took 1.28 to 2.83, and leaving them out gained 5.6 us, while having them on POOL cost 6.5 more than on DVE (seven_places_pool against seven_places), where the eight take 5.5 us of busy time.
- **The last pair, +0.9, and small edits, +0.6.** The stage of w_out took 1.6 us more than before (94.8 from 1021.6 to 1116.4, against 93.2), at the split into `hl`, which the sum doesn't have. By first_rows_early its place or its turn in the queue is the reason; in the changed kernel ACT also stands 7.23 us at a page of w_up in front of it, and these were not told apart. Whether the order of the last pair cost its 0.9 was not tried by itself. w_out's blocks 6 and 7 came in time, as said.
- **"DVE 48.4 of 54.5: enough, if inputs come in time."** no_low_parts bears this out; the condition was the matter. I summed busy times of engines that take their queues in order, and the sum says nothing of who stands in front of whom.

The range, 1713.5 to 1726, held neither miss. It was built from the heads' rival alone; the slower one was kept out by the mean share.
